# A two-layer hybrid mixer backbone on one core: when shared PSUM tiles are read, and the order of its work

## The chip, the cores and the metric

The kernel runs on one core of a Trainium2 chip. The metric is device time in microseconds, from a run of the whole kernel in one launch; less is better. Engines are named as in the profile: PE is TensorE (matmul), PEld its weight loads, DVE is VectorE, ACT is ScalarE, POOL is GpSimd, SP the engine whose queue issues the transfers.

## The reference

512 latent tokens and 256 context tokens, 1024 wide, pass two layers. Each layer is a set of four token mixers behind one input projection, and then an MLP:

```python
hx = modulate(rms_norm(x, norm1_g[l]), mod_x[0], mod_x[1])
zx = jnp.split(hx @ w_in[l], N_PARTS, axis=-1)          # 10 parts, 256 wide
...
y_a = conformer_conv(a_val, a_gate, conv_w, ...)        # GLU, 31-tap depthwise conv, layer norm, silu
y_b = diff_attention(q1, q2, k1, k2, v, lam, ...)       # softmax(q1 k1) - lam softmax(q2 k2), 4 heads
y_c = spatial_gating(u, sv, ...)                        # gelu, layer norm, 128x128 mixing of tokens
y_d = short_conv_mixer(bg, cg, xin, conv_w)             # 3-tap conv between two gates
x = x + mod_x[2] * (jnp.concatenate([y_a, y_b, y_c, y_d], axis=-1) @ w_out[l])
x = x + mod_x[5] * (jnp.square(jax.nn.relu(h @ w1[l])) @ w2[l])
...
return rms_norm(x, final_g)
```

The six modulation vectors come from `silu(c) @ ada_w[l] + ada_b[l]`. The context goes through the same weights in layer 0; layer 1 needs of it only keys and values. All is fp32.

## The kernel before, in words

Channels lie on the 128 partitions, tokens along the free dimension: 768 tokens (512 latent, 256 context) in layer 0, 512 in layer 1. Every weight chunk `raw` (128 x 1024) is loaded on SP's queue and split in two: ACT casts the high part `wh` to fp32r, DVE subtracts it to get the low part `wl`. Activations are split in the same way (`hh` and `hl`, `ffh` and `ffl`, and so on). A product is three matmuls, high x high, low x high and high x low (`mm3`).

The order of the instructions is made by a planner inside the kernel's Python (`class Plan`). Each kind of work is a generator; `turn` hands out an engine by the number that the kind has in `PRIO` (the lower goes first), and the planner's clocks, latencies and due times say when a generator goes on. What comes out is one fixed list of instructions per engine. Waits on semaphores are added from the tiles that instructions read and write, and each engine then runs its list in order.

The stages are these.

- Mixers of layer 0: the chunks of the input projection in the order `W_ORDER[0]`, pairs (part, half). Parts 0 and 1 are the value and gate of the convolution, 2, 3 and 4 are q, k and v, 5 and 6 are u and sv of the spatial gating, 7, 8 and 9 are bg, cg and xin of the short convolution. On PE these are matmuls into tiles `w`, `tm` and, for three chunks at a time, `pair`. The convolution is 31 DVE instructions per half (`ca`). Attention starts when q, k and v are there: `score` matmuls, DVE minimum and ACT exponential (`e`), normalization, transposes by PE (`tp`, line L1282), `pv`. The output projection `wo` is laid between them.
- MLP of layer 0: the 32 hidden tiles of w1 and w2 are done in groups (`GROUPS[0]`). The first group is plain: 8 products of 128 channels per hidden tile over 768 tokens. The other groups use seven products in place of eight on 2 x 2 blocks (two hidden tiles, two halves of the channels, two halves of 384 tokens each): one pass of `seven_products` makes two hidden tiles.
- Mixers and MLP of layer 1, in the same way but plain throughout, and the last norm.

In one pass of `seven_products`, products 1 and 6 go to the two halves of one PSUM tile of 1024 columns (`sa`: columns 0 to 383 and 512 to 895), products 7 and 5 to those of a second (`sb`), products 2, 4 and 3 to tiles of their own (`sg`, `sc`, `sh`). The sums over them are generators of their own: `sum_p` is ACT's copy of product 1 into `sx`, `sum_q` adds product 6 to it on DVE, `sum_r` adds product 7, `sum_c22` product 5, and `sum_c11`, `sum_c21`, `sum_c12` the other three; each result goes through relu, square and the split into `ffh` and `ffl`. Ahead of the stage `sums` makes the summed token operands (`t2`, `t3`) and, when the plain group's w1 products are done, overwrites half of `hh` and `hl` for product 5.

Of the adaptive modulation, blocks (`ada_block`, tile `am`) and rows (`ada_row`, tile `dump`) are strewn over the run at the distances `ADA_GAP`.

Of the kernel before, what the change touches and what calls it, by code (L numbers as in the profile page):

```python
# [26 lines left out]
PADW = 15 + NL + 15 + NC + 15  # L27
RESERVE = 1
N_ATT = 12
ADA_GAP = (7000.0, 6000.0, 9000.0, 4500.0, 5500.0)  # L30
ROWS = ('pe', 'pe', 'pv', 'pv')
ADA_NS = 600.0
ADA_PS = 'pv'
# [5 lines left out]
WS_POOL = 3500.0  # L39
SV_POOL = 1300.0  # L40
LASTK = 1
H_KEEP = 6
UNIT_B = 3000.0
X_PAD = 3
N_MORE = 0
SPILL = (4, 5)
SAVE_GAP = 3000.0
SLACK = 300.0
BALANCE = 6000.0
LATE5 = 0  # L50
WO2 = ('s', 'acc')
N_E = 4
LAT = {"pe": 200.0, "dve": 150.0, "act": 160.0, "pool": 80.0, "dma": 0.0}
CTX_LAG = 3
PE0, DVE0, DMA0 = 3300.0, 2600.0, 2600.0
WARM_N = 512
WARM_END = 10000.0
# [1 line left out]
START = ('g0', 'p', 'x', 'h0', 'w', 'g1', 'h1', 'c', 'h2', 'g2', 'g3', 'h3', 'q')  # L59
ROW0 = ("vp", "vv", "vp", "vv", "vp", "vv", "vp", "vv")  # L60
N_WT = 4
GROUPS = ((4, 6, 6, 6, 6, 4), (8, 8, 8, 8))
HALF = NT // 2
N_RAW, N_ARAW = 2, 1 if MEM else 2

# [3 lines left out]
GELU_S = math.sqrt(2.0 / math.pi)  # L69
SQ_D = 32.0 ** -0.5  # L70
K_OUT = [1, 0, 6, 5, 7, 4, 2, 3]
W_ORDER = ([(0, 0), (1, 0), (3, 0), (8, 0), (0, 1), (3, 1), (1, 1), (9, 0), (4, 0), (7, 0), (8, 1), (6, 0), (5, 0), (2, 0), (5, 1), (9, 1), (7, 1), (2, 1)], [(0, 1), (1, 0), (0, 0), (1, 1), (5, 1), (2, 0), (5, 0), (3, 0), (6, 0), (8, 1), (2, 1), (8, 0), (4, 0), (9, 1), (9, 0), (7, 0), (3, 1), (7, 1)])


PRIO = {'weight_split': 10, 'pe_main': 50, 'ada_row': 56, 'ada_rest': 52, 'ada_block': 5, 'conv_dve': 15, 'conv_pool': 43, 'conv_norm': 47, 'ev_aval': 23, 'ev_agate': 5, 'ev_cg': 39, 'ev_xin': 19, 'ev_bg': 8, 'ev_u': 17, 'ev_sv': 55, 'ev_v': 17, 'ev_qk': 2, 'attention': 22, 'attn_sub': 49, 'attn_unit': 3, 'attn_pv': 44, 'attn_norm': 34, 'residual': 2, 'residual_ap': 30, 'split_y': 4, 'norm_third': 12, 'norm_split': 12, 'on_pool': 18, 'affine': 13, 'ev_ff': 13, 'add_tile': 24, 'final_norm': 24, 'group': 30, 'ada_start': 28, 'ada_turn': 30, 'startup': 22, 'warm': 49, 'cond_bcast': 35, 'row_start': 48, 'on_dve': 8, 'pair_split': 20, 'half_rest': 5, 'sums': 28, 'rectified': 12, 'sum_p': 4, 'sum_q': 48, 'sum_r': 43, 'sum_c11': 44, 'sum_c22': 34, 'sum_c21': 33, 'sum_c12': 26}


SLOW = {"dve": 0.5, "pool": 0.25}
# [11 lines left out]
class Plan:  # L90
# [18 lines left out]
    def spawn(self, gen, at=None, prio=None):  # L109

        if gen not in self.prio:
            self.prio[gen] = PRIO.get(gen.__name__, self.current) if prio is None else prio
        self.seq += 1
# [127 lines left out]
def hybrid_dit_kernel(  # L241
# [524 lines left out]
    def chunk():  # L766

        i = nxt["i"]
        nxt["i"] += 1
        return i  # L770
# [134 lines left out]
    def norm_tiles(h, ss, t0, n, s, gain, shift, mod_ev, kind):  # L905
# [13 lines left out]
        def make(k):  # L919
            if h[k].made is None:  # L920
                h[k].made = Ev()
                yield r_buf.get(2, H_KEEP)
                h[k].make("h")
# [52 lines left out]
    for l in range(DEPTH):  # L976
        for part, hf in W_ORDER[l]:
            order.append([w_in[l, part * 2 + hf]])
# [6 lines left out]
        f0 = 0  # L985
        for g, nf in enumerate(GROUPS[l]):
            if l == 0 and g > 0:
# [18 lines left out]
    def free_ring(i):  # L1006
        wt_.pop(i)
        r_ring.put(1, P.clock["pe"])
# [5 lines left out]
    def mixers(L):  # L1014
# [233 lines left out]
        def attn_unit(pair, hh, qt, k0, kn, wt, qi, done):  # L1248
# [15 lines left out]
            yield t  # L1264
            if P.load("act") + P.load("pool") + UNIT_B < 2 * P.load("dve"):
                t = yield from act(e[1][:, 0:kn], e[1][:, 0:kn], AF.Copy, scale=rs[:, 1:2])
# [7 lines left out]
            r_att.put(1, t)  # L1274
            yield t + SLACK
            for k3 in range(0, nk, 3):
# [66 lines left out]
        def attn_pv(pair, qts, kblk, wts, done, nfree, last_ev):  # L1343
            for ev in done:
                yield ev
            yield P.now + SLACK
            yield r_pv.get()
# [168 lines left out]
        def first_two():  # L1516
# [7 lines left out]
            for c in cs:  # L1524
                yield wev[c]
            for i in range(8 + CTX_LAG):
                for (t0, n), k in zip(segs, (i, i - CTX_LAG)):
                    if not 0 <= k < 8:
# [16 lines left out]
        else:  # L1545
            for part, hf in W_ORDER[l][0:3]:
                yield from before(part, hf)
            yield from together([chunk() for _ in range(3)], h, [(0, 256), (256, 256)], lambda j, p_, t0, n, put: (
                ev_aval, ev_agate)[W_ORDER[l][j][0]](W_ORDER[l][j][1], p_, t0, n, lambda n, t: put(t)))
        for part, hf in W_ORDER[l][2 if l == 0 else 3:]:  # L1550
            if (part, hf) == (3, 0):
# [32 lines left out]
            yield from before(part, hf)  # L1584
            if (part, hf) == W_ORDER[l][-1]:
                P.fire(L.h_done)
# [3 lines left out]
            ps = []  # L1590
            if LASTK and (part, hf) == W_ORDER[l][-1]:
                for _ in spans:
# [220 lines left out]
    def seven_products(L, ff):  # L1813

        LO, HI = slice(0, HALF), slice(HALF, NT)
        h2 = L.h2
        yield L.sums_ev
        third = lambda k: slice((k % 2) * HALF, (k % 2 + 1) * HALF)
        token = {
            1: lambda k: (h2[k].hi[:, LO], h2[k].lo[:, LO]),  # L1820
            2: lambda k: (h2[k + 4].hi[:, LO], h2[k + 4].lo[:, LO]),
            3: lambda k: (h2[k + 4].hi[:, HI], h2[k + 4].lo[:, HI]),
            4: lambda k: tuple(x[:, LO] for x in L.t2[k]),
            5: lambda k: (h2[k].hi[:, HI], h2[k].lo[:, HI]),
            6: lambda k: tuple(x[:, HI] for x in L.t2[k]),
            7: lambda k: tuple(x[:, third(k)] for x in L.t3[k // 2]),
        }
        waits = {4: 4, 5: 1, 6: 2, 7: 3}
        at = {"n": 0, "c": None}

        def product(p, out):
            if at["n"] % 2 == 0:
                at["c"] = chunk()
            c, o = at["c"], at["n"] % 2
            at["n"] += 1
            yield hev[c, o]
            wh, wl = wt_[c]
            for k in range(4):
                if p in waits:
                    yield L.t_ev[k, waits[p]]  # L1840
                hi, lo = token[p](k)
                t = yield from mm3(out, wh[:, 4 * o + k], wl[:, 4 * o + k], hi, lo, k == 0, k == 3)
            if o or at["n"] == 7 * (len(ff) // 2):
                free_ring(c)
            return t

        for i in range(0, len(ff), 2):
            S = Layer()
            S.ev = {n: Ev() for n in ("p", "q", "y", "r", "u")}
            S.left = {ff[i]: 2, ff[i + 1]: 2}  # L1850
            yield r_s.get()
            p_ = acc_tile("s", "sa")
            S.a, S.b = p_[:, 0:HALF], p_[:, 512:512 + HALF]
            yield r_buf.get()
            S.x = buf([128, NT], name="sx")
            t = yield from product(1, S.a)
            P.spawn(sum_p(S), t)
            t = yield from product(6, S.b)
            P.spawn(sum_q(S), t)
            yield r_buf.get(3, True)  # L1860
            S.y = buf([128, NT], name="sy")
            ff[i].make("ff")
            yield r_acc.get()
            S.g = acc_tile("acc", "sg")[:, 0:HALF]
            t = yield from product(2, S.g)
            P.spawn(sum_c11(S, ff[i]), t)
            yield r_s.get()
            p_ = acc_tile("s", "sb")
            S.c, S.d = p_[:, 0:HALF], p_[:, 512:512 + HALF]
            t = yield from product(7, S.c)  # L1870
            P.spawn(sum_r(S), t)
            t = yield from product(5, S.d)
            yield r_buf.get(3, True)
            S.z = buf([128, NT], name="sz")
            ff[i + 1].make("ff")
            P.spawn(sum_c22(S, ff[i + 1]), t)
            yield r_acc.get()
            S.e = acc_tile("acc", "sc")[:, 0:HALF]
            t = yield from product(4, S.e)
            P.spawn(sum_c21(S, ff[i + 1]), t)  # L1880
            yield r_acc.get()
            S.h = acc_tile("acc", "sh")[:, 0:HALF]
            t = yield from product(3, S.h)
            P.spawn(sum_c12(S, ff[i]), t)
# [84 lines left out]
    def mlp(L, nxt_layer):  # L1969
# [6 lines left out]
        seven = l == 0  # L1976
        for g, nf in enumerate(GROUPS[l]):
            fin = g == len(GROUPS[l]) - 1
            ff = [Act() for _ in range(nf)]
# [195 lines left out]
    def ada_rest():  # L2175
# [14 lines left out]

        yield from rows(0, (2,), ROWS[0], ADA_GAP[0], (0, 1))
        t = yield from ada_fin(0, 16, 24, (0, 1))
        P.fire(L0.gate_ev[2], t)
        yield from rows(0, (3, 4), ROWS[1], ADA_GAP[1], (0, 1))
        t = yield from ada_fin(0, 24, 40, (0, 1))
        P.fire(L0.mod2_ev, t)
        if LATE5:
            yield L0.mlp_ev
        yield from rows(0, (5,), ROWS[2], ADA_GAP[2], (0, 1))
        t = yield from ada_fin(0, 40, 48, (0, 1))  # L2200
        P.fire(L0.gate_ev[5], t)
        yield L0.h2[0].ev[2]
        yield from rows(1, (0, 1), ROWS[3], ADA_GAP[3], (0, 1))
        t = yield from ada_fin(1, 0, 16, (0, 1))
        P.fire(L1.mod1_ev, t)
        yield from rows(1, (2, 3, 4, 5), "v", ADA_GAP[4], (0,))
        t = yield from ada_fin(1, 16, 48, (0,))
# [85 lines left out]
```

## Time and profile before

| | us |
|---|---|
| median of 3 runs | 1520.59 (1519.42 to 1521.8) |
| profiled execution | 1520.49 |
| its span | 1518.5 |
| PE busy in the span | 1455.6 |
| DVE busy | 1067.1 |
| ACT busy | 621.2 |
| POOL busy | 84.5 |

The span runs from the first to the last instruction of the profile. In it layer 0's mixers take until about 365 us, its plain MLP group until 440, the seven-product groups until 906 and layer 1's mixers until 1160; then layer 1's MLP runs to the end. Rows of the profile name line, engine, operation and tiles as out<-in; a number in brackets is the idle time of the engine before the row and what ended it. L364 is the matmul, L304 DVE's two-tensor operation, L309 its scalar-tensor-tensor operation, L342 ACT's copy or cast, L337 its activation.

### The profile page before, as it was taken

What the parts mean: (1) busy time and instruction counts of PE and PEld (TensorE: products, weight loads), DVE (VectorE), ACT (ScalarE), POOL (GpSimd) and SP (SyncE); (2) the same over time, 40 slices, a digit from 0 to 9 for tenths busy, and PEclk for the clock granted to TensorE, in tenths of its full rate; (3) what the DMA queues carried; (4) which work ended last, traced back from release to release, by engine and by line L of the source; (5) the groups of instructions that cost most, each with busy time, mean ns of one, the idle gap of its engine ahead of it and who ended that gap; (6) DMA issues with size and microseconds to landing.
All of it is one profiled execution on the core that took longest, in us unless ns stands there. A gap on an engine that the chain in (4) does not pass through costs nothing.

```text
span 1518.5 us, 22138 instructions
## 1 busy us (share of the span) xinstructions
PE 1455.6 (96%) x8500; PEld 1253.4 (83%) x8500; DVE 1067.1 (70%) x1939; ACT 621.2 (41%) x1165; POOL 84.5 (6%) x94
## 2 busy tenths in 40 slices
PE   8999999999999999999999999989998999999997
PEld 4788887779888898888888888877678888888887
DVE  4899779979998687685775567999878434333343
ACT  4421436745436144252351445325655324132342
POOL 0000103220000000000000000102110000000000
PEclk9999999999999999999999999999999999999999
DMA  9565367321233434434442124542511333223321
GB/s 320 193 224 172 102 188 230 99 71 48 70 93 101 133 111 141 145 110 157 127 136 87 49 80 156 164 147 84 160 57 67 100 98 97 97 98 98 97 98 56
DMA packets 71369, 184.51 MB, mean 122 GB/s; under 512 B 9056, under 2 KB 18016, under 8 KB 71264
## 3 DMA queue, kind: packets, MB, share of 16 engines
q1 hardware_dynamic: 71264, 183.10, 37.3%
q8 instruction: 67, 1.10, 0.3%
q14 instruction: 38, 0.31, 0.1%
HBM read 168.91 MB, written 14.16 MB: 121 GB/s over the span
## 4 chain that ended last, share of the span: by engine, by line
PE 67%; DVE 11%; ACT 1%; issue 1%; DMA 1%; POOL 1%; DVEq 0%; POOLq 0%; ACTq 0%
PE w L364 40%; PE wo L364 6%; PE sa L364 4%; PE pair L364 4%; PE sb L364 3%; DVE wl L304 2%; PE sc L364 2%; PE sh L364 2%; DVE ca L309 2%; PE sg L364 2%; PE pv L364 1%; PE score L364 1%; PE tp L1282 1%; DVE x L309 1%; DVE nu L309 1%
## 5 line engine op out<-in xcount | busy, mean ns | idle before, releaser
L342 ACT CAST wh<-raw 128x1024 fp32r<-128x1024 f32 (+2 forms) x242 | 208.8, 869 | 495.3 <-PE w L364 403.0
L304 DVE TENSOR_TENSOR wl<-raw,wh 128x1024 fp32r<-128x1024 f32 (+2 forms) x242 | 240.6, 1001 | 128.6 <-ACT wh L342 125.1
L364 PE MATMUL w<-ffh,wh 128*128 128x512 f32 (+1 forms) x792 | 276.9, 350 | 3.5 <-DVE x L309 2.3
L364 PE MATMUL w<-ffl,wh 128*128 128x512 f32 (+1 forms) x792 | 276.8, 350 | 0.5 <-DVE ffl L304 0.5
L364 PE MATMUL w<-ffh,wl 128*128 128x512 f32 (+1 forms) x792 | 276.4, 349 | 0.0
L364 PE MATMUL w<-hh,wh 128*128 128x512 f32 (+1 forms) x624 | 230.4, 369 | 0.7 <-ACT yu L342 0.7
L364 PE MATMUL w<-hl,wh 128*128 128x512 f32 (+1 forms) x624 | 229.6, 368 | 0.3 <-DVE hl L309 0.3
L364 PE MATMUL w<-hh,wl 128*128 128x512 f32 (+1 forms) x624 | 229.3, 367 | 0.0
L309 DVE SCALAR_TENSOR_TENSOR x<-w,md,x 128x512 f32<-128x512 f32 (+1 forms) x132 | 83.6, 635 | 182.2 <-PE w L364 181.7
L364 PEld LDWEIGHTS w<-ffh,wh 128*128 128x128 f32 x792 | 149.8, 189 | 24.6 <-DVE x L309 3.3
L364 PEld LDWEIGHTS w<-ffl,wh 128*128 128x128 f32 x792 | 149.8, 189 | 20.0 <-DVE ffl L304 0.8
L364 PEld LDWEIGHTS w<-ffh,wl 128*128 128x128 f32 x792 | 149.7, 189 | 19.5
L364 PEld LDWEIGHTS w<-hh,wl 128*128 128x128 f32 x624 | 118.3, 190 | 21.6 <-issue 3.3
L364 PEld LDWEIGHTS w<-hh,wh 128*128 128x128 f32 x624 | 118.2, 190 | 21.1 <-issue 2.1
L364 PEld LDWEIGHTS w<-hl,wh 128*128 128x128 f32 x624 | 118.3, 190 | 20.0 <-issue 1.6
L309 DVE SCALAR_TENSOR_TENSOR ca<-gpad,sm,ca 128x783 f32<-128x783 f32 (+1 forms) x120 | 106.6, 888 | 1.6
L596 DVE CUSTOM_DVE_ANT_0 dump<-raw,cbt 128x1024 bf16<-128x1024 f32 x80 | 97.8, 1222 | 6.7 <-DMA raw<-adaT 6.5
L347 POOL TENSOR_TENSOR rr<-rs,few 128x2 f32<-128x2 f32 (+1 forms) x30 | 27.5, 918 | 1129.6 <-DVE rs L317 1129.6
L337 ACT ACTIVATE e<-e,mx 128x768 f32<-128x768 f32 (+1 forms) x80 | 67.9, 849 | 26.5 <-DVE e L1240 26.2
L1240 DVE TENSOR_SCALAR_CACHE_REDUCE e<-score 128x768 f32<-128x768 f32 (+1 forms) x80 | 65.9, 845 | 2.4 <-PE score L364 2.0
L364 PE MATMUL wo<-yl,wh 128*128 128x512 f32 (+1 forms) x144 | 53.4, 371 | 2.4 <-DVE yl L304 2.4
L364 PE MATMUL wo<-yh,wh 128*128 128x512 f32 (+1 forms) x144 | 53.6, 372 | 1.4 <-ACT zr L342 1.4
(237 smaller groups left out, 2718.9 us busy)
## 6 DMA issues: line engine op xcount, KB each, us to landing
raw<-w SPq DMA_DIRECT2D x96, 512.0 KB, 3.5
raw<-adaT SPq DMA_DIRECT2D x56, 512.0 KB, 3.4
raw<-w_in SPq DMA_DIRECT2D x40, 512.0 KB, 4.5
ab<-adaB SPq DMA_DIRECT2D x24, 384.0 KB, 6.4
raw<-wo SPq DMA_DIRECT2D x16, 512.0 KB, 3.7
raw<-w SPq DMA_DIRECT2D x32, 256.0 KB, 2.6
a<-adaB SPq DMA_DIRECT2D x16, 384.0 KB, 7.2
raw<-w SPq DMA_DIRECT2D x16, 384.0 KB, 3.2
```

Source lines behind the costliest of these rows:

```text
L304: nc.vector.tensor_tensor(out=out, in0=in0, in1=in1, op=op)
L309: nc.vector.scalar_tensor_tensor(out=out, in0=in0, scalar=s, in1=in1, op0=op0, op1=op1)
L337: nc.scalar.activation(out=out, in_=in_, func=func, scale=scale, **kw)
L342: nc.scalar.copy(out, in_)
L347: nc.gpsimd.tensor_tensor(out=out, in0=in0, in1=in1, op=op)
L364: nc.tensor.matmul(out, lhsT, rhs, start=start, stop=stop)
L596: nc.vector.tensor_tensor_reduce(out=dump, in0=raw, in1=cbt[s], op0=ALU.mult, op1=ALU.add, scale=1.0, scalar=0.0, accum_out=md[l][:, s, r: ...
L1240: nc.vector.tensor_scalar(out=e[:, 0:kn], in0=s_[:, k0:k0 + kn], scalar1=-SQ_D, scalar2=None, op0=ALU.mult, op1=ALU.min, accum_out=mx)
L1282: nc.tensor.transpose(tp[:, j * 128:(j + 1) * 128], e[0][:, (k3 + j) * 128:(k3 + j + 1) * 128], id_sb)
```

## The change

In `seven_products`, `sum_p` is started when product 6 is done, no longer when product 1 is, and `sum_r` when product 5 is, no longer when product 7 is. Beside it numbers of the planner are replaced.

```diff
-ADA_GAP = (7000.0, 6000.0, 9000.0, 4500.0, 5500.0)
+ADA_GAP = (7000.0, 4000.0, 9000.0, 4500.0, 5500.0)
-H_KEEP = 6
-UNIT_B = 3000.0
+H_KEEP = 7
+UNIT_B = 6000.0
-SLACK = 300.0
+SLACK = 0.0
-CTX_LAG = 3
+CTX_LAG = 2
-GROUPS = ((4, 6, 6, 6, 6, 4), (8, 8, 8, 8))
+GROUPS = ((6, 6, 6, 6, 4, 4), (8, 8, 8, 8))
-W_ORDER = (..., [(0, 1), (1, 0), (0, 0), (1, 1), (5, 1), (2, 0), (5, 0), (3, 0), (6, 0), ...])
+W_ORDER = (..., [(1, 1), (1, 0), (0, 0), (2, 0), (3, 0), (5, 0), (0, 1), (8, 0), (8, 1), ...])
-PRIO = {'weight_split': 10, 'pe_main': 50, ..., 'ev_agate': 5, ..., 'attention': 22, ..., 'sum_q': 48, ...}
+PRIO = {'weight_split': 10, 'pe_main': 57, ..., 'ev_agate': 4, ..., 'attention': 2, ..., 'sum_q': 20, ...}
@@ seven_products
-            t = yield from product(1, S.a)
+            yield from product(1, S.a)
+            t = yield from product(6, S.b)
             P.spawn(sum_p(S), t)
-            t = yield from product(6, S.b)
             P.spawn(sum_q(S), t)
...
-            t = yield from product(7, S.c)
+            yield from product(7, S.c)
+            t = yield from product(5, S.d)
             P.spawn(sum_r(S), t)
-            t = yield from product(5, S.d)
```

The numbers mean: `ADA_GAP` the distance between modulation blocks in ns; `H_KEEP` how many buffers a normalization leaves free; `UNIT_B` when an attention tile's normalization goes to ACT and POOL in place of POOL and DVE (as many take each way in both programs); `SLACK` by how much the planner holds back an attention tile's transposes and `pv`; `CTX_LAG` by how many channel tiles the context follows the latent tokens in the first two chunks; the first group of layer 0's MLP is now 6 tiles and the two last are 4. In layer 0's chunk order v comes third after the first two chunks and not seventh. 13 passes of `seven_products` remain of 14.

What that does to the lists of instructions is shown at three places. The first is PE's list in the second pass of `seven_products`, within product 6 (`t2h`, `t2l` are its token operand, a wait stands in brackets with the engine waited for). Before:

```order
L364 MATMUL sa<-t2h,wl 128x384
L364 MATMUL sa<-t2h,wh 128x384
L364 MATMUL sa<-t2l,wh 128x384
L364 MATMUL sa<-t2h,wl 128x384 [waits Activation_49]
L364 MATMUL sa<-t2h,wh 128x384
```

Now, from the product's first matmul on:

```order
L364 MATMUL sa<-t2h,wh 128x384 [waits Activation_49]
L364 MATMUL sa<-t2l,wh 128x384
L364 MATMUL sa<-t2h,wl 128x384 [waits DVE_49]
L364 MATMUL sa<-t2h,wh 128x384
L364 MATMUL sa<-t2l,wh 128x384
```

The wait for ACT inside the product is no longer there; waits stand at its first matmul and at its first use of the weight's low part.

The second place is ACT's list at the start of layer 1's mixers, behind the first three chunks (`tg` is the tanh of the convolution's gate, `yu` is u, `zr` a piece of q or k on its way to the rotary, `qkh` its high part). Before:

```order
L342 CAST wh<-raw 128x1024
L342 COPY aval<-pair 128x256
L342 CAST wh<-raw 128x1024 x2
L342 COPY yu<-w 128x512
L342 CAST wh<-raw 128x1024
L337 ACTIVATE tg<-pair 128x256 x2
```

Now:

```order
L342 COPY aval<-pair 128x256
L342 CAST wh<-raw 128x1024
L342 COPY zr<-w 128x512
L342 CAST wh<-raw 128x1024
L342 COPY zr<-w 128x512
L342 CAST wh<-raw 128x1024
L342 COPY zr<-w 128x256
L342 CAST qkh<-zr 128x256
L337 ACTIVATE tg<-pair 128x256 x2
```

The pieces of q and k have moved ahead of the gate's tanh, and u behind it.

The third place is DVE's list where layer 1's first normalized tile is made (`nu` is the normalized tile, `hl` its low part after modulation, `x` the residual of layer 0's last MLP chunks). Before:

```order
L309 SCALAR_TENSOR_TENSOR nu<-x_2643,gain_1_87,sq 128x256
L304 TENSOR_TENSOR wl<-raw,wh 128x1024
L309 SCALAR_TENSOR_TENSOR x_2661<-w_9024,md_84,x_2661 128x256
L304 TENSOR_TENSOR wl<-raw,wh 128x1024
L309 SCALAR_TENSOR_TENSOR nu<-x_2646,gain_1_87,sq 128x256
L309 SCALAR_TENSOR_TENSOR hl<-nu,md_85,hh 128x256
```

Now:

```order
L309 SCALAR_TENSOR_TENSOR nu<-x_2583,gain_1_87,sq 128x256
L304 TENSOR_TENSOR wl<-raw,wh 128x1024
L309 SCALAR_TENSOR_TENSOR x_2601<-w_8996,md_84,x_2601 128x256
L309 SCALAR_TENSOR_TENSOR hl<-nu,md_85,hh 128x256 x2
L304 TENSOR_TENSOR wl<-raw,wh 128x1024
```

The second weight split has moved from ahead of `hl` to behind it.

More of the change, by code (lines that the diff above doesn't have):

```diff
@@ L71 @@
 K_OUT = [1, 0, 6, 5, 7, 4, 2, 3]
-W_ORDER = ([(0, 0), (1, 0), (3, 0), (8, 0), (0, 1), (3, 1), (1, 1), (9, 0), (4, 0), (7, 0), (8, 1), (6, 0), (5, 0), (2, 0), (5, 1), (9, 1), (7, 1), (2, 1)], [(0, 1), (1, 0), (0, 0), (1, 1), (5, 1), (2, 0), (5, 0), (3, 0), (6, 0), (8, 1), (2, 1), (8, 0), (4, 0), (9, 1), (9, 0), (7, 0), (3, 1), (7, 1)])
-PRIO = {'weight_split': 10, 'pe_main': 50, 'ada_row': 56, 'ada_rest': 52, 'ada_block': 5, 'conv_dve': 15, 'conv_pool': 43, 'conv_norm': 47, 'ev_aval': 23, 'ev_agate': 5, 'ev_cg': 39, 'ev_xin': 19, 'ev_bg': 8, 'ev_u': 17, 'ev_sv': 55, 'ev_v': 17, 'ev_qk': 2, 'attention': 22, 'attn_sub': 49, 'attn_unit': 3, 'attn_pv': 44, 'attn_norm': 34, 'residual': 2, 'residual_ap': 30, 'split_y': 4, 'norm_third': 12, 'norm_split': 12, 'on_pool': 18, 'affine': 13, 'ev_ff': 13, 'add_tile': 24, 'final_norm': 24, 'group': 30, 'ada_start': 28, 'ada_turn': 30, 'startup': 22, 'warm': 49, 'cond_bcast': 35, 'row_start': 48, 'on_dve': 8, 'pair_split': 20, 'half_rest': 5, 'sums': 28, 'rectified': 12, 'sum_p': 4, 'sum_q': 48, 'sum_r': 43, 'sum_c11': 44, 'sum_c22': 34, 'sum_c21': 33, 'sum_c12': 26}
+W_ORDER = ([(0, 0), (1, 0), (3, 0), (0, 1), (4, 0), (1, 1), (8, 0), (3, 1), (5, 0), (9, 0), (6, 0), (7, 0), (8, 1), (2, 0), (9, 1), (5, 1), (7, 1), (2, 1)], [(1, 1), (1, 0), (0, 0), (2, 0), (3, 0), (5, 0), (0, 1), (8, 0), (8, 1), (5, 1), (6, 0), (4, 0), (9, 0), (7, 0), (2, 1), (9, 1), (3, 1), (7, 1)])
+PRIO = {'weight_split': 10, 'pe_main': 57, 'ada_row': 56, 'ada_rest': 12, 'ada_block': 19, 'conv_dve': 15, 'conv_pool': 18, 'conv_norm': 38, 'ev_aval': 55, 'ev_agate': 4, 'ev_cg': 3, 'ev_xin': 30, 'ev_bg': 18, 'ev_u': 42, 'ev_sv': 61, 'ev_v': 34, 'ev_qk': 31, 'attention': 2, 'attn_sub': 49, 'attn_unit': 19, 'attn_pv': 52, 'attn_norm': 39, 'residual': 2, 'residual_ap': 58, 'split_y': 18, 'norm_third': 12, 'norm_split': 10, 'on_pool': 38, 'affine': 4, 'ev_ff': 51, 'add_tile': 13, 'final_norm': 21, 'group': 15, 'ada_start': 1, 'ada_turn': 5, 'startup': 45, 'warm': 16, 'cond_bcast': 25, 'row_start': 0, 'on_dve': 59, 'pair_split': 10, 'half_rest': 50, 'sums': 60, 'rectified': 15, 'sum_p': 58, 'sum_q': 20, 'sum_r': 29, 'sum_c11': 51, 'sum_c22': 55, 'sum_c21': 41, 'sum_c12': 9}
 SLOW = {"dve": 0.5, "pool": 0.25}
```

## The prediction

> **What bounds the kernel now.** I read the page first. The profiled execution took 1520.49 us, 2.0 us more than its span and 0.1 us under the median of the three runs shown (1520.59), so a change of the span can be taken off either.
>
> ```profile
> span 1518.5 us, 22138 instructions
> PE 1455.6 (96%) x8500; PEld 1253.4 (83%) x8500; DVE 1067.1 (70%) x1939; ACT 621.2 (41%) x1165; POOL 84.5 (6%) x94
> ```
>
> TensorE is busy nearly all the time, so only its idle time, its slow-clocked time and the number of its matmuls can move the end. The view by windows, cut at the stages, says where that idle time is.
>
> ```profile
> core 0: us, PE busy (x) PEld busy (x) DVE busy (x) ACT busy (x) POOL busy (x), PEclk, DMA share, GB/s
> 205.00:365.00 160.00, 153.66 (x1025) 126.00 (x1023) 140.44 (x325) 92.25 (x204) 35.48 (x32) 1.00 0.42 132
> 440.00:873.00 433.00, 412.57 (x2323) 379.02 (x2322) 305.72 (x524) 166.44 (x309) 0.00 (x0) 1.00 0.36 117
> 906.00:1160.00 254.00, 236.95 (x1432) 200.30 (x1431) 221.00 (x420) 127.31 (x246) 33.45 (x37) 0.95 0.38 121
> ```
>
> The first row is attention and output projection of layer 0, the second the seven-product stage, the third layer 1's mixers. The seven-product stage has the most idle time, 20.4 us; layer 1's mixers have 17.1 us and a clock of 0.95. The waits of PE inside 440 to 873 us account for the 20.4:
>
> ```profile
> PE sa L364 <- ACT sx L342: 8.0, 14, 0.6
> PE sb L364 <- DVE sx L304: 7.8, 12, 0.7
> PE w L364 <- DVE x L309: 2.3, 2, 1.2
> PE sb L364 <- DVE hl L304: 2.0, 2, 1.5
> ```
>
> Each of the 14 passes of the stage waits once in tile sa for ScalarE's copy into sx, and 12 wait in sb for VectorE's sum into sx. Tile sa holds products 1 and 6, sb products 7 and 5. The timeline of one pass shows what a wait is:
>
> ```profile
> 657.73 0.33 PE L364 MATMUL sa<-t2h,wl 128*128 128x384 f32 x1
> 657.90 0.34 PE L364 MATMUL sa<-t2h,wh 128*128 128x384 f32 x1
> 658.81 0.45 PE L364 MATMUL sa<-t2l,wh 128*128 128x384 f32 x1 [0.57 <-ACT sx L342]
> ...
> 666.03 0.33 PE L364 MATMUL sb<-hh,wh 128*128 128x384 f32 x1
> 666.20 0.34 PE L364 MATMUL sb<-hl,wh 128*128 128x384 f32 x1
> 667.19 0.44 PE L364 MATMUL sb<-hh,wl 128*128 128x384 f32 x1 [0.65 <-DVE sx L304]
> ```
>
> ```profile
> 658.28 0.48 ACT L342 COPY sx<-sa 128x384 f32<-128x384 f32 x1 [0.25 <-PE sa L364]
> ...
> 666.58 0.56 DVE L304 TENSOR_TENSOR sx<-sb,sx 128x384 f32<-128x384 f32 x1 [0.30 <-PE sb L364]
> ```
>
> Matmuls normally start 0.17 us apart; here 0.91 and 0.99 us pass. The copy reads the first half of sa at 658.28, while product 6 is already filling the second half, and the next matmul into sa waits until that read is over, though it writes other columns.
>
> **The change part by part.** *Reads after both products.* In PE's order the wait in the middle of product 6 is gone (first place shown in the change); what stays is at its start, for the token operand, and at the weight's low part. Per pass sa loses 0.91 - 0.17 = 0.74 us and sb 0.99 - 0.17 = 0.82 us: 14 x 0.74 + 12 x 0.82 = 20.2 us. The ends of the range are the idle time of the matmul rows, 8.0 + 7.8 = 15.8 us, and that of the weight loads:
>
> ```profile
>   PEld sa L364: 12.4, 14
> ...
>   PEld sb L364: 11.6, 12
> ```
>
> 24.0 us. I take 20.2, from the starts, since throughput goes by starts.
>
> What is late next: the copy and the first sum come one product later (12 matmuls, 2.1 us). Product 2's sum needs the copy, but product 2 itself still runs for 2.1 us, against 0.48 us of copy; the sums of products 4 and 3 need the first sum of sb, and those products run 4.1 us against 0.56 + 2 x 0.56 us of sums. sa is wanted again only a pass later. At the end of the last group, of 4 tiles, the chain has w2 from 873.0, and the timeline the last low part of a hidden tile:
>
> ```profile
> 873.03 30.80 PE w L364 x190
> ...
> 875.32 0.56 DVE L304 TENSOR_TENSOR ffl<-sy,ffh 128x384 fp32r<-128x384 f32 x1 [0.63 <-ACT ffh L342]
> ```
>
> That low part follows product 3, which is not moved; it is done at 875.9 and first used 24 matmuls of w2, some 4 us, after product 3. So the delay costs 0; were the cover gone, 1 us at each of five group ends, which I keep for the range.
>
> The Trainium skill ("PSUM — Partial Sum Buffer", Summary: rules for kernel authors) asks only that a read under a running matmul goes to a different bank, and gives a bank 512 fp32 columns. By it, halves at columns 0 and 512 would need no wait at all, and an early read would be free; the trace has the wait, so here the measurement decides against the free read. The same list says to evacuate promptly, which speaks against the change: by it 13 passes x 2 halves x 2.1 us of later reading could cost up to 55 us if the next tile were waiting for them, where the sum has 0.
>
> *A larger first group.* 6 instead of 4 hidden tiles go through the plain group, so 13 passes remain. In the chain of waits:
>
> ```profile
> 601.26 37.83 PE w L364 x216
> 662.55 4.00 PE sb L364 x23
> ```
>
> A plain matmul costs 37.83 / 216 = 0.175 us, a seven-product one 4.00 / 23 = 0.174. A plain pair of tiles has 96 of them, a pass 84: 16.8 - 14.6 = +2.2 us on PE, which nothing hides. It gives back two things. The plain w2 waits at its start:
>
> ```profile
> 406.06 0.50 PE L364 MATMUL w<-ffh,wh 128*128 128x512 f32 x1 [0.94 <-DVE ffh L322]
> ...
> 452.50 0.44 PE L364 MATMUL sb<-hl,wh 128*128 128x384 f32 x1 [1.48 <-DVE hl L304]
> ```
>
> With two more tiles to accumulate ahead of the last one, 6 matmuls of 512 columns or 1.4 us, the first wait (1.1 us by starts, and the 0.8 us that follow it for the low part) goes: -1.9 us. The second is VectorE rewriting token operands for product 5; these are made while the plain group runs, which is now 2 x 16.8 us longer: -1.9 us (the row's 1.48 and 0.5 us in the pass). Ends: 0 and -4.
>
> *SLACK 0.* The planner no longer leaves 0.3 us between an attention tile and its transposes. 40 units x 0.3 us = 12 us is the far end, 0 the near one:
>
> ```profile
> PE tp L1282 <- DVE e L309: 0.8, 2, 0.4
> ```
>
> Only two transposes waited, so most have room, and PE has projection matmuls in the same place: +1.
>
> *New orders, layer 1.* The trio that starts layer 1's projections still holds both gates that the convolution needs, but next come q and k instead of another value chunk and u. In ScalarE's order (second place) the gate's tanh, tg, stood behind u's copy and now stands behind three copies zr for the rotary. The gate is about as late as before, but VectorE gets the rotary work ahead of it. In the trace VectorE stands still here:
>
> ```profile
> DVE wl L304 <- ACT wh L342: 11.1, 5, 4.9
> ...
> 944.17 0.58 ACT L342 COPY yu<-w 128x512 f32<-128x512 f32 x1 [4.61 <-PE w L364]
> 945.60 0.66 ACT L337 ACTIVATE tg<-pair 128x256 f32<-128x256 f32 x2
> ...
> 958.03 0.73 DVE L1175 STREAM_SHUFFLE shf<-zr 128x512 f32<-128x512 f32 x1
> 959.31 1.79 DVE L304 TENSOR_TENSOR zr<-zr,rope 128x512 f32<-128x512 f32 x1
> 961.68 0.68 DVE L304 TENSOR_TENSOR zr<-zr,shf 128x512 f32<-128x512 f32 x1
> ```
>
> Two shuffles, two rotary products, two sums and two and a half splits of the length of a sum move into the 11.1 us: 1.5 + 1.8 to 3.6 + 1.4 + 1.7, less 1.4 us of u's gelu that moves out, is some 5 us. VectorE is what this stage's PE waits for later:
>
> ```profile
> PE score L364 <- DVE e L1240: 5.6, 3, 4.8
> PE pair L364 <- DVE hl L309: 4.4, 4, 2.1
> ```
>
> and the longest of these waits is followed by a halved clock:
>
> ```profile
> 1019.00:1024.00 5.00, 0.50 (x3) 0.07 (x1) 5.00 (x7) 1.14 (x2) 0.00 (x0) 0.98 0.89 313
> 1024.00:1031.00 7.00, 6.71 (x17) 5.38 (x18) 6.97 (x14) 2.99 (x5) 1.59 (x1) 0.52 0.23 88
> ```
>
> 7 us at 0.52 lose 3.4 us. VectorE earlier by 5 us takes away the 4.8 us wait, of which the stage, being VectorE's, may ask part again later: -5.
>
> The first normalized tile of layer 1 gains too.
>
> ```profile
> 909.38 1.22 DVE L304 TENSOR_TENSOR wl<-raw,wh 128x1024 fp32r<-128x1024 f32 x1
> ```
>
> In VectorE's order (third place) this split now stands behind hl instead of ahead of it; PE's wait for hl, 2.1 us at the longest, shrinks, but soon needs that split: -1. Against it, counted in PE's order, 70 instead of 58 projection matmuls of 512 columns stand behind the last score, where PE is no longer held up:
>
> ```profile
> 1173.65 323.38 PE w L364 x1436
> ```
>
> 12 x 0.225 = +2.7. And with the wait the clock drop of 3.4 us may go; I count half, -1.7. Layer 1: -5 - 1 + 2.7 - 1.7 = -5, ends -12 and +7 (all four terms good; or none, with one more drop of the clock and its wait).
>
> *New orders, layer 0.* Counted in PE's order, 181 projection matmuls stand behind the last score instead of 235, so 54 are done between the scores, where PE's idle time is 6.3 us at most; the tail of attention has less work to hide behind. I take -2, ends -6 and +6.
>
> *Moved transfers.* Weight chunks, the q and k round trips and the ada blocks (spaced closer now) change places on SP's queue. PE's only listed wait for a transfer is
>
> ```profile
> PE am L439 <- DMA a<-adaB: 0.9, 1, 0.9
> ```
>
> in the start, whose loads stand as before: 0.
>
> **The sum.** 1520.5 - 20.2 + 2.2 - 1.9 - 1.9 + 1 - 5 - 2 = 1492.7, say 1493.
>
> **Rivals.** (a) The waits go, but the new orders give some back: layers 0 and 1 at their bad ends (+13 in place of -7) make 1513, at half that way 1503. For it: VectorE is busy 221 of 254 us in layer 1's mixers, and a new order moves its work rather than removing it. Against it: the 11.1 us of idle time that is filled.
> (b) The wait only changes its place: the weight splits are just in time (the order has a wait for DVE in product 6 in 9 of 13 passes), so PE, faster by 20 us, runs into them. That gives back up to the 20.2: 1513. Against it: VectorE has 127 of 433 us free in the stage, and PE never waited for a split there.
> (c) Slower: attention in layer 1 stalls PE in several places past the point at which the clock drops. An idle stretch as long as the 4.8 us one costs 4.8 + 3.4 = 8.2 us; it decides from four more of them on, 1493 + 33 = 1526. The Trainium skill ("TensorE: Matmul & The Clock Gate", What's actually happening) has the same rule, half clock after an idle window of about 3.4 us; the trace agrees, with 0.52 behind 4.8 us and 1.00 throughout the stage of 0.6 us waits. Against it: the trace has one such stretch.
>
> **How the numbers follow.** Forecast 0.78 (1482 to 1502), (a) at 1503 to 1513 0.12, (b) 0.06, (c) 0.03, and 0.01 for no net change. The low end, 1482, is the layers' good ends; the high end, 1507, reaches into (a) until under 2 in 10 is left out. Faster by over 0.2%, about what a measurement of this kernel can tell from no change (3 us), is all but (c) and the last: 0.96; within it 0.01; slower 0.03.
>
> **What would show it.** Right: no PE wait for sx in the seven-product stage, its PE idle time under 5 us; no wait near the first plain w2; VectorE's idle time behind layer 1's first trio halved; a single drop of the clock, or none, inside layer 1's attention. Wrong: PE waits for wl or hl in sa and sb, or more scores that wait for e behind new clock drops.

## The result, and the profile after

| | before | after |
|---|---|---|
| median of 4 runs, us | 1520.81 (1519.42 to 1521.8) | 1486.37 (1484.44 to 1486.9) |
| ratio, 95% interval | | 0.9772 (0.9755 to 0.9789) |
| span of the profiled execution, us | 1518.5 | 1484.5 |

The change makes the kernel 34.4 us faster; 1493 was forecast, with a range from 1482 to 1507. The first two lines of the page now read:

```profile
span 1484.5 us, 22137 instructions
PE 1449.4 (98%) x8512; PEld 1253.8 (84%) x8512; DVE 1056.7 (71%) x1924; ACT 611.9 (41%) x1151; POOL 76.9 (5%) x94
```

TensorE does 12 matmuls more and its idle time has fallen from 62.9 to 35.1 us. To see where, I cut both executions at the same landmarks: the starts of the first matmul into tile `pair` of each MLP or mixer stage. The lengths between them:

| us | layer 0 mixers | layer 0 MLP | layer 1 mixers | layer 1 MLP | span |
|---|---|---|---|---|---|
| before | 362.7 | 546.3 | 240.5 | 369.0 | 1518.5 |
| after | 362.0 | 517.6 | 235.1 | 369.8 | 1484.5 |
| difference | -0.7 | -28.7 | -5.4 | +0.8 | -34.0 |

So 28.7 of the 34.0 us came in the MLP of layer 0, and 5.4 in layer 1's mixers. The view by windows of the kernel after, over attention and output projection of layer 0, the seven-product stage (466 to 846) and layer 1's mixers:

```profile
205.00:365.00 160.00, 156.89 (x1033) 128.20 (x1032) 137.68 (x319) 92.10 (x204) 31.05 (x33) 1.00 0.42 132
466.00:846.00 380.00, 379.71 (x2187) 356.98 (x2186) 276.66 (x479) 153.39 (x291) 0.00 (x0) 1.00 0.38 122
877.00:1125.00 248.00, 235.39 (x1421) 196.51 (x1421) 217.38 (x416) 125.08 (x244) 31.73 (x37) 0.97 0.38 124
```

In the seven-product stage TensorE's idle time is 0.3 us in 380, where it was 20.4 in 433. All waits of PE between 362 and 846 us, so the plain group included, are these, and none names sx, a token operand of the stage, or sa or sb:

```profile
PE pair L364 <- ACT rl L337: 1.0, 2, 0.5
PE pair L364 <- DVE wl L304: 0.9, 1, 0.9
PE w L364 <- DVE ffl L304: 0.4, 1, 0.4
PE pair L364 <- DVE x L309: 0.3, 1, 0.3
```

One pass in the timeline of the kernel after: product 1 goes over into product 6 at 594.56 at the usual distance of 0.17 us, and the copy into sx stands behind product 6, the first sum of sb behind product 5.

```profile
594.39 0.33 PE L364 MATMUL sa<-hh,wl 128*128 128x384 f32 x1
594.56 0.33 PE L364 MATMUL sa<-t2h,wh 128*128 128x384 f32 x1
...
597.62 0.46 ACT L342 COPY sx<-sa 128x384 f32<-128x384 f32 x1
...
603.08 0.56 DVE L304 TENSOR_TENSOR sx<-sb,sx 128x384 f32<-128x384 f32 x1 [0.21 <-PE sb L364]
```

The copy starts 1.2 us after the last matmul of product 6 has started (596.47), and no matmul waits for it.

Layer 1's mixers between their landmarks, before and after (two views by windows):

```profile
909.00:1149.50 240.50, 225.15 (x1359) 188.91 (x1357) 208.32 (x390) 118.37 (x229) 31.84 (x35) 0.96 0.39 126
```

```profile
879.60:1114.70 235.10, 224.18 (x1359) 186.16 (x1358) 206.51 (x391) 117.74 (x228) 30.12 (x35) 0.99 0.40 129
```

The matmuls are the same 1359. Idle time fell from 15.4 to 10.9 us and the mean clock rose from 0.96 to 0.99. The clock record has three stretches at half clock in the stage before (from 911.2 for 3.4 us, from 1023.8 and 1071.6 for 6.8 us each) and one after (from 1031.9, 6.8 us). The waits of PE there in the kernel after:

```profile
PE score L364 <- DVE e L1240: 3.0, 3, 1.8
...
PE pair L364 <- DVE hl L309: 1.1, 3, 0.5
```

The 4.8 us wait of a score is down to 1.8, and the 2.1 us wait for hl to 0.5.

### The profile page after: what moved, and what is told of

It is laid out like the page before. It is cut to its first block, busy times and chain, and to the rows that moved or that the text cites. A ratio compares the mean times of both kernels' runs of the same rounds, so it can differ in the third digit from the quotient of the medians.

```text
span 1484.5 us, 22137 instructions
## 1 busy us (share of the span) xinstructions
PE 1449.4 (98%) x8512; PEld 1253.8 (84%) x8512; DVE 1056.7 (71%) x1924; ACT 611.9 (41%) x1151; POOL 76.9 (5%) x94
## 4 chain that ended last, share of the span: by engine, by line
PE 86%; DVE 9%; DMA 2%; issue 1%; ACT 1%; SPq 0%; DVEq 0%; POOLq 0%; ACTq 0%
PE w L364 53%; PE wo L364 7%; PE sa L364 4%; PE sb L364 4%; PE pair L364 4%; PE tm L364 2%; PE sh L364 2%; PE sc L364 2%; PE sg L364 2%; DMA a<-adaB 2%; PE pv L364 2%; PE tp L1282 2%; DVE wl L304 2%; PE score L364 1%; DVE ca L309 1%; DVE e L1240 1%
## 5 line engine op out<-in xcount | busy, mean ns | idle before, releaser
L364 PE MATMUL w<-hh,wh 128*128 128x512 f32 (+1 forms) x656 | 239.5, 365 | 0.4 <-ACT hh L337 0.4
L364 PE MATMUL w<-hl,wh 128*128 128x512 f32 (+1 forms) x656 | 239.1, 364 | 0.7 <-DVE hl L309 0.7
L364 PE MATMUL w<-hh,wl 128*128 128x512 f32 (+1 forms) x656 | 238.3, 363 | 0.0
L364 PEld LDWEIGHTS w<-hh,wh 128*128 128x128 f32 x656 | 123.8, 189 | 22.7 <-issue 2.4
L364 PEld LDWEIGHTS w<-hl,wh 128*128 128x128 f32 x656 | 123.8, 189 | 21.4 <-issue 1.7
L364 PEld LDWEIGHTS w<-hh,wl 128*128 128x128 f32 x656 | 123.7, 189 | 19.0 <-issue 0.4
L364 PE MATMUL wo<-yh,wl 128*128 128x512 f32 (+1 forms) x144 | 53.4, 371 | 0.0
```

Source lines behind the costliest of these rows:

```text
L364: nc.tensor.matmul(out, lhsT, rhs, start=start, stop=stop)
```

## The experiments

Eleven kernels were timed, each against the kernel before on the same chip. Their stages, cut at the same landmarks of their profiled executions:

| | edit | median us | ratio, 95% interval | layer 0 mixers | layer 0 MLP | layer 1 mixers |
|---|---|---|---|---|---|---|
| e1 | before + late reads | 1491.26 | 0.9802 (0.9783 to 0.9821) | 363.4 | 519.8 | 237.2 |
| e2 | after, early reads | 1514.76 | 0.9959 (0.9944 to 0.9973) | 361.6 | 543.9 | 237.5 |
| e3 | before, halves crossed | 1497.91 | 0.9851 (0.9834 to 0.9868) | 364.3 | 527.8 | 235.8 |
| e4 | after, old groups | 1504.50 | 0.9892 (0.9876 to 0.9907) | 361.6 | 534.1 | 236.2 |
| e5 | after, old order in layer 1 | 1483.08 | 0.9747 (0.9731 to 0.9763) | 362.1 | 517.6 | 234.3 |
| e6 | before, new order in layer 1 | 1536.28 | 1.0093 (1.0073 to 1.0114) | 363.7 | 546.2 | 255.8 |
| e7 | after, SLACK 300 | 1489.84 | 0.9795 (0.9765 to 0.9825) | 366.0 | 521.4 | 231.0 |
| e8 | e4 + early `sums` | 1493.43 | 0.9817 (0.9802 to 0.9832) | 360.6 | 523.2 | 236.5 |
| e9 | e1 + new PRIO | 1491.28 | 0.9810 (0.9794 to 0.9825) | 362.1 | 520.1 | 236.8 |
| e10 | e1 + attention's PRIO | 1562.44 | 1.0278 (1.0261 to 1.0294) | 393.9 | 522.8 | 275.3 |
| e11 | e1 + evictions' PRIO | 1494.92 | 0.9834 (0.9816 to 0.9851) | 364.7 | 521.7 | 239.6 |

**The reads.** e1 takes the two edits of `seven_products` into the kernel before and nothing else; e2 takes them out of the kernel after.

```diff
 # e1: the kernel before with
-            t = yield from product(1, S.a)
+            yield from product(1, S.a)
+            t = yield from product(6, S.b)
             P.spawn(sum_p(S), t)
...
-            t = yield from product(7, S.c)
+            yield from product(7, S.c)
+            t = yield from product(5, S.d)
             P.spawn(sum_r(S), t)
```

> The kernel before with the two edits of seven_products alone; all numbers of the planner as before, so that the mixers of layer 0 stand as before up to the first pass. Theory A (the waits inside tiles sa and sb are the price, 24 us by the idle time of the weight loads): 1520.8 - 24 = 1497, the stage from first sa to last sh 24 us shorter, no PE wait for sx. Rival B (the new orders made part of the stage's gain): no more than 16 us, 1505. Rival C (the splits are just in time and take the place of the waits): 1515 or more, with PE waits for wl in sa or sb.

> The changed kernel with the two reads put back to where they were before; all new numbers stay. Theory A: 13 passes instead of 14, 13 x 0.85 + 13 x 0.93 = +23 us, 1509, with the waits for sx back. Rival B: +10 us or less, 1496, since the new orders would keep reads and products apart.

e1 measured 1491.26 against 1520.61 on the same chip, 29.4 us faster, where the sum had 20.2 for these waits and 1.9 for the wait for hl. So these two edits alone bring 29 of the change's 34 us. From the first matmul into sa to the last into sh the stage went from 434.1 to 407.7 us; another 3.3 us came in layer 1's mixers, which e1 leaves as they were. The window of e1 over the stage shows 1.7 us of idle time:

```profile
440.00:847.00 407.00, 405.30 (x2326) 380.34 (x2325) 304.21 (x525) 164.39 (x309) 0.00 (x0) 1.00 0.39 125
```

e2 is the mirror: 28.4 us slower than after, the same stage 400.4 instead of 374.1 us, with the waits back in it:

```profile
PE sb L364 <- DVE sx L304: 7.9, 12, 0.7
PE sa L364 <- ACT sx L342: 6.9, 12, 0.6
PE w L364 <- DVE x L309: 3.4, 2, 2.3
```

What one wait costs is more than the prediction took. It took the step to the waiting matmul, which starts at 658.81, 0.91 us behind the last one instead of 0.17. But the matmul behind it is late as well:

```profile
659.09 0.34 PE L364 MATMUL sa<-t2h,wl 128*128 128x384 f32 x1
```

It starts 0.28 us later, not 0.17. A wait in sa therefore costs 0.85 us, one in sb 0.93, and the 26 waits 14 x 0.85 + 12 x 0.93 = 23.1 us. That is nearer to the idle time of the weight loads (24.0) than to the starts (20.2) or the idle time of the matmuls (15.8). In e2 12 + 12 waits are 21.4 us by it; with the 3.4 us for x and one stretch of 3.4 us at half clock (1.7 lost) that makes 26.5, and 26.3 was measured.

**Is it the early read, or the tile that it shares?** e3 keeps the early reads of the kernel before and lays the products differently: 1 and 7 in one tile, 6 and 5 in the other, so that product 6 runs in a tile that nobody reads. (Both tiles are taken when the pass starts, and each is given back behind its last read.)

```diff
-            p_ = acc_tile("s", "sa")
-            S.a, S.b = p_[:, 0:HALF], p_[:, 512:512 + HALF]
+            pa, pb = acc_tile("s", "sa"), acc_tile("s", "sb")
+            S.a, S.c = pa[:, 0:HALF], pa[:, 512:512 + HALF]
+            S.b, S.d = pb[:, 0:HALF], pb[:, 512:512 + HALF]
...
-            p_ = acc_tile("s", "sb")
-            S.c, S.d = p_[:, 0:HALF], p_[:, 512:512 + HALF]
...
```

> The kernel before, with early reads as before, but products 1 and 7 share one tile and products 6 and 5 the other, so that the product that runs while a sum is read writes another tile. If the guard goes by tile (theory A), early reads cost nothing then: no wait for sx inside a product and 1497, as with the reads after both products. If an early read under a running matmul costs by itself (rival D: the banks or the engines get in each other's way): no better than 1515.

1497.91: the waits for sx shrink from 15.8 us to 0.8, with the reads as early as ever. Both tiles are now held from the pass's start, and other waits come in:

```profile
PE w L364 <- DVE x L309: 3.0, 1, 3.0
PE sb L364 <- DVE x L309: 1.8, 4, 0.4
PE sb L364 <- ACT wh L342: 1.1, 1, 1.1
PE sb L364 <- ACT sx L342: 0.5, 1, 0.5
PE sa L364 <- DVE sx L304: 0.3, 1, 0.3
```

So the guard goes by the tile and not by the columns, and an early read beside a running matmul costs next to nothing if the tiles differ. The Trainium skill ("PSUM — Partial Sum Buffer", Summary: rules for kernel authors) asks for no more than a different bank; e3 agrees with it, at 0.8 us of waits for sx, while the kernel before, whose halves lie at columns 0 and 512, waits 15.8 us all the same. The prediction took those waits for a measurement against the free read. They are not one: the program sets them itself, by semaphores for whole tiles.

**The larger first group.** e4 gives the kernel after the old sizes. e8 is e4 with the priority of `sums`, which makes t2, t3 and product 5's operands, back at its old value.

```diff
 # e4
-GROUPS = ((6, 6, 6, 6, 4, 4), (8, 8, 8, 8))
+GROUPS = ((4, 6, 6, 6, 6, 4), (8, 8, 8, 8))
 # e8: beside it, in PRIO
-'sums': 60
+'sums': 28
```

> The changed kernel with the groups of before (4, 6, 6, 6, 6, 4): one pass more, one plain pair less. By the count of matmuls alone -2.2 us, 1484. By the prediction's steps the waits at the first plain w2 (1.9 us) and for hl in product 5 (1.9 us and more) come back, so that it ends about 2 us above the changed kernel, 1488.

> The run with the old groups again (4 plain tiles first, 14 passes), with one priority set back: the work that makes the token operands for the seven products, sums, from 60 (last of all) to 28 as in the kernel before. If the 18 us that the old groups cost in the changed kernel are the waits for t2h and hl and the halved clocks behind them, since sums comes last and the shorter plain group does not cover it, they go: 1485, or 1484 by one plain pair less. If the longer plain group is worth 18 us by itself: 1504 again.

e4 was expected at 1484 to 1488 and came out at 1504.50, the plainest miss. Its waits of PE in the MLP of layer 0 begin with

```profile
PE sa L364 <- ACT t2h L342: 6.1, 1, 6.1
PE sb L364 <- DVE hl L304: 3.6, 1, 3.6
```

and it has three stretches at half clock (13.7 us together). The new priority makes `sums` late, and 6 tiles of plain work cover that where 4 do not. e8 says so: both waits vanish and 11.1 us of the 18.1 come back. Of the remaining 7.1 us 5.6 lie in the same stage, first of all at the first plain w2 matmul,

```profile
PE w L364 <- DVE ffh L322: 4.1, 1, 4.1
```

with a stretch of 3.4 us at half clock behind it. So the group's size is not worth the 1.6 us that the sum gave it: it is the cover for other new numbers, which cost 18 us without it. 11 of them are shown to be the priority of `sums`; which numbers make the other 7 wasn't tested.

**SLACK.**

```diff
 # e7: the kernel after with
-SLACK = 0.0
+SLACK = 300.0
```

> The changed kernel with the planner's 300 ns ahead of transposes and pv again. The prediction gave SLACK 0 a cost of 1 us, so 1485.4; its far end of 12 us would give 1474. If the changed priorities were chosen with SLACK 0 in mind, another order of attention can cost a few us, 1490.

1489.84, 3.5 us slower than after, though its interval reaches over after's ratio. In the profiled execution layer 0's mixers take 4.0 us more and its plain group 3.9 more, layer 1's mixers 4.1 less. Of PE's waits between 221 and 366 us the largest is new:

```profile
PE tp L1282 <- ACT wt L342: 1.6, 1, 1.6
```

So it is with the 0.3 us of room that a transpose waits for wt; with SLACK 0 none does. The feared cost of no slack isn't there in this execution.

**The order of layer 1.** e5 gives the kernel after layer 1's old chunk order, e6 the kernel before its new one.

```diff
 # e5, layer 1; e6 is the reverse, in the kernel before
-[(1, 1), (1, 0), (0, 0), (2, 0), (3, 0), (5, 0), (0, 1), (8, 0), (8, 1), ...]
+[(0, 1), (1, 0), (0, 0), (1, 1), (5, 1), (2, 0), (5, 0), (3, 0), (6, 0), ...]
```

> The changed kernel with layer 1's chunk order of before; layer 0 and all other numbers stay as changed. Theory A (q and k ahead of the gate fill VectorE's idle time behind the first trio): VectorE stands still some 11 us there again in place of about 8, layer 1's mixers take 240 us instead of 235, 1491. Rival E (the 5 us came from halved clocks that happen to be fewer, two in place of three and a half): the stage moves by the number of drops, 1.7 or 3.4 us each, whatever VectorE's idle time is; 1486 with the same drops.

> The kernel before with layer 1's chunk order of the changed one, and no other number. Theory A: layer 1's mixers 5 us shorter, 1515.5. Rival E: the waits of the matmuls change by under 2 us and the time follows the number of halved clocks. Rival F (the order of chunks works only with the new priorities): no gain, 1521.

Both went against my account. e5 is not slower but 3 us faster than after (the intervals overlap a little; it is the fastest version run). Layer 1's mixers take 234.3 us there, with VectorE's idle time behind the first trio back. The waits of DVE from 850 to 930 us, after first and then e5:

```profile
DVE wl L304 <- ACT wh L342: 5.4, 3, 4.5
DVE shf L1175 <- ACT zr L342: 2.6, 1, 2.6
```

```profile
DVE wl L304 <- ACT wh L342: 12.8, 6, 4.9
```

So after fills 11.1 us of idle time down to 8.0, which is not half, since the rotary itself now waits for ScalarE, and e5 does without.

e6 is slower than before by 15 us, although the idle time is filled as the prediction wanted (DVE, 880 to 960 us):

```profile
DVE wl L304 <- ACT wh L342: 6.0, 3, 4.5
```

What e6 pays stands in PE's waits of the stage,

```profile
PE score L364 <- DVE e L1240: 11.1, 5, 8.4
```

and in the windows from the first score to the last, of the kernel before and of e6:

```profile
1016.10:1114.60 98.50, 90.45 (x480) 69.50 (x479) 88.30 (x169) 60.50 (x120) 18.51 (x19) 0.93 0.39 126
```

```profile
1007.40:1136.40 129.00, 116.23 (x613) 87.56 (x612) 101.78 (x189) 65.03 (x124) 21.25 (x19) 0.93 0.35 113
```

With q and k ahead the first score comes 9.6 us sooner behind the stage's start (97.5 us, not 107.1), and what has not been done by then stands among the scores: 133 more matmuls, and 13.5 us more of VectorE's work (101.8 for 88.3 us). The scores wait for VectorE 11.1 us instead of 5.6, and stretches at half clock of 17.1 and 10.2 us go with it. So filling the idle time that VectorE had before the first score does not by itself shorten this stage; as far as e6 shows, what VectorE has to do among the scores matters more.

**The priorities.** If the order doesn't bring layer 1's gain, the priorities might. e9 puts all but those of the MLPs and of the last norm into e1, e10 attention's alone, e11 those of the projection's evictions and the convolution alone.

```diff
 # e10: e1 with, in PRIO
-'attention': 22, 'attn_unit': 3, 'attn_pv': 44, 'attn_norm': 34
+'attention': 2, 'attn_unit': 19, 'attn_pv': 52, 'attn_norm': 39
 # e11: e1 with, in PRIO
-'ev_qk': 2, 'ev_cg': 39, 'ev_aval': 23, 'conv_pool': 43, 'conv_norm': 47, ...
+'ev_qk': 31, 'ev_cg': 3, 'ev_aval': 55, 'conv_pool': 18, 'conv_norm': 38, ...
```

> The kernel before with the late reads of e1 and, beside them, the new kernel's PRIO for everything but the MLP's kinds (sums, sum_*, rectified, ev_ff and a few that didn't change); chunk orders, groups, SLACK and H_KEEP as before. Theory G, that layer 1's gain comes from the priorities whatever the order of chunks: its mixers, 237.2 us in e1, take 233 to 235 us, and the whole some 3 us less than e1's 1491.3, 1486 to 1489. Theory H, that priorities gain only together with the new GROUPS, SLACK and orders: mixers of layer 1 at 237 or more, the whole at 1491 or above.

> As e1, with only the new PRIO of attention (22 to 2, its normalization 3 to 19, attn_pv 44 to 52, attn_norm 34 to 39). If attention being let ahead of the other work on VectorE is what gains, layer 1's mixers fall from e1's 237.2 to 234 or 235 us, and the waits of scores for e shrink; if not, they stay within 1 us of 237.2.

> As e1, with only the new PRIO of the projection's evictions and of the convolution (ev_cg 39 to 3, ev_aval 23 to 55, ev_qk 2 to 31, conv_norm 47 to 38, conv_pool 43 to 18 and the like). If these gain, layer 1's mixers fall from e1's 237.2 to 234 or 235 us; if attention's priority is the one that gains, they stay within 1 us of 237.2, or grow, since q and k are let ahead of less work.

e9 ends where e1 ends, 1491.28 against 1491.26, so theory G falls: beside the late reads, with the old orders and groups, these priorities bring nothing on the whole. e10, expected to gain 2 or 3 us, loses 71. The windows over the scores of both layers, e1 first and then e10:

```profile
222.90:324.80 101.90, 97.56 (x626) 76.17 (x625) 93.16 (x222) 68.51 (x156) 30.56 (x28) 1.00 0.47 148
991.00:1091.90 100.90, 94.90 (x521) 74.47 (x521) 90.38 (x171) 62.27 (x122) 19.75 (x19) 0.98 0.39 128
```

```profile
221.00:360.00 139.00, 126.35 (x715) 99.22 (x714) 107.83 (x243) 71.27 (x160) 27.08 (x27) 0.90 0.40 128
1024.00:1153.00 129.00, 113.99 (x545) 84.09 (x543) 94.25 (x175) 64.65 (x124) 20.00 (x19) 0.88 0.34 108
```

The idle time of TensorE goes from 4.3 to 12.7 us and from 6.0 to 15.0, and the clock from 1.00 and 0.98 to 0.90 and 0.88. The same four numbers stand in the kernel after, where layer 0's scores take 100.3 us. e11 alone loses 4 us; its layer 1 waits in other places:

```profile
PE sp L364 <- DVE sv L304: 8.2, 3, 4.8
```

e9 holds both sets beside the rest of the priorities and loses nothing, so something in it makes up for attention's loss. Whether that is e11's set isn't shown. One local gain can be put down to the rest of e9's set: the first trio of layer 1's projections (from the stage's first matmul to the 144th into `pair`) takes 23.9 us before, 25.5 in e1 and 24.3 in e11, but 22.6 in e9 and e5 and 21.9 after. In the first three PE stands idle for 2.1 us at the first matmul with hl, and half clock follows; before, the row is

```profile
911.44 0.58 PE L364 MATMUL pair<-hl,wh 128*128 128x256 f32 x1 [2.07 <-DVE hl L309]
```

In e9, as after, the longest such wait is 0.5 us.

## Why the prediction was right, and where its terms were not

- *Waits for sx, -20.2.* The mechanism is shown by e1, e2 and e3. The size was too small: 23.1 us, since a wait also delays the matmul behind it. The choice of the starts among the three ends was the weak step; the weight loads' 24.0 were nearer.
- *What the sum left standing.* The two waits of w for x in the stage (2.3 us idle, 2.5 by starts) are gone after, one of them (1.2) still stands in e1. The sum had nothing for them.
- *Operands of product 5, -1.9.* The wait is gone, and by starts it was worth 3.0 us. But e1, with 4 plain tiles, has lost all but 0.8 us of it: the later reads do most of this, and the larger group isn't the main reason.
- *Larger plain group, +2.2.* By the usual distance of each kind of matmul (the median between its start and the next, such as 0.227 us for 512 columns), TensorE's work from the start of layer 0's MLP to its end went from 508.0 to 510.2 us, +2.1. The wait at the first plain w2 fell from 0.9 + 0.5 to 0.4 us; by starts that is a gain of 1.3 us where 1.9 was taken. What was missed is that the group covers the new place of `sums` (e4, e8).
- *The stage together.* 23.1 + 3.0 + 2.5 + 1.3 - 2.1 = 27.8 of the 28.7 us; the other 0.9 are not told apart.
- *SLACK, +1.* Wrong in sign as far as e7 goes (3.5 us gained); the interval is too wide to call it shown.
- *Layer 1, -5.* It measured -5.4, but the reason was wrong, so that the match is luck. VectorE's filled idle time is no gain: without it the stage is as fast (e5, 234.3 us), and the kernel before with it is 15 us slower (e6). Two smaller steps held: the first normalized tile (-1 taken, the first trio is 2.1 us shorter), and the longer tail behind the last score (+2.7 taken; from the last score to the MLP it went from 34.9 to 37.7 us). The gain itself lies in the clock drops, of which the sum had counted only -1.7. At the usual distances the stage's 1359 matmuls take 218.7 us. What it took beyond that, waits included, was 21.9 us before, 9.1 of them inside the stretches at half clock (17.1 us long together), and 16.4 us after, 3.9 of them inside (6.8 us long). So 5.2 of the 5.4 us lie in those stretches, and outside them 12.8 us became 12.5. In e6 it is the same the other way: 23.3 us lie inside, 14.2 more than before, of its 15.3. What took the drops away is shown for the first alone, which came with the wait for hl of 2.07 us: after, e5 and e9 have no such wait and no drop there, e1 and e11 have both. The rest can be chance in part: one execution of each kernel was profiled, e1 has 3.3 of the 5.4 us with no edit in layer 1's numbers, and kernels with the same chunk order and priorities of layer 1 as after lie between 235.1 and 237.5 us (e2, e4, e8).
- *Layer 0, -2.* It was -0.7 us.
- *The rivals.* No give-back (a) and no just-in-time splits (b): the only wait for a weight split in the MLP is 0.9 us in the plain group. (c) did not come, but e6 and e10 are that case: parts of the change's numbers without the rest bring it about, so that its chance hung on the numbers fitting together, for which the profile before had no row.

Against the span the sum had 27.8 us and 34.0 were measured. The 6.2 us between them are 6.9 us in the MLP of layer 0, where the sum was too small, 0.4 in layer 1's mixers, and against them 0.3 us in layer 0's mixers (SLACK counted there) and 0.8 in the last MLP.

## What to carry to other kernels

Where two products share a tile and one of them is read while the other runs, count the wait once per pass and price it by the starts of the waiting matmul and of the one behind it; here the idle time of the weight loads came close to that (24.0 for 23.1 us), that of the matmuls did not (15.8). Reading both halves at the end, or laying the two products into different tiles, removes the wait for a few lines of code, if nothing needs the later read for a whole product. Priorities and orders of a planned schedule are to be tested as a set: parts of this one cost 15 us (layer 1's order alone) and 71 us (attention's priorities alone), and the set without its larger group loses 18 us, though the whole set is 5 us faster than the late reads by themselves (the intervals overlap a little). And an explanation that has only its size to show for it, as that of layer 1's 5 us, hasn't been proved: the run that takes the part out is what tells.

## What the runs showed of the hardware

The clock drops after less idle time than I had assumed. In e4 it halves at 406.6 us, behind these two:

```profile
405.00 0.51 PE L364 MATMUL w<-ffh,wh 128*128 128x512 f32 x1 [1.32 <-DVE ffh L322]
405.99 0.51 PE L364 MATMUL w<-ffl,wh 128*128 128x512 f32 x1 [0.49 <-DVE ffl L304]
```

In the kernel before the same place, with 0.94 and 0.49 us, kept the full clock. The Trainium skill ("TensorE: Matmul & The Clock Gate", What's actually happening) speaks of an idle window of about 3.4 us; in e4 both waits and what lies between them take 2.3 us (403.68 to 405.99). The prediction found the trace in agreement by its 4.8 us wait, and passed over the wait of 2.07 us up to 911.44, within which half clock sets in as well (from 911.2). The amount of idle time alone doesn't decide it: waits of 0.52 and 1.48 us between 448.8 and 452.5 us of the kernel before kept the full clock. These are single cases, and no threshold can be read off them. All stretches at half clock inside the stages lasted 3.4 us or about a multiple of it (6.8, 10.2, 13.7, 17.1, 23.9), in every kernel. What that costs is large where it adds up: between the start and the last norm e10 has 99.0 us at half clock and e1 17.1. If half of that time is lost, it is up to 41 of the 71 us between them, an estimate.
